# Turning the banded heads' probabilities by DMA transposes instead of TensorE, in a hybrid attention layer

## The chip, the cores and the metric

The kernel runs on one core of one Trainium2 chip. The metric is the device time of one execution in microseconds. The profile is of one such execution, taken by the hardware profiler; stated times are from runs of the kernel by itself.

## The reference

One decoder layer, 2048 positions of width 1024. The input is normalised, modulated and projected once; eight heads do attention over all earlier positions with a forget gate ("forgetting heads", mixer A), eight heads do attention within a band of 128 positions with a learned sink ("banded heads", mixer B, two key/value heads). Both are gated, concatenated, projected, normalised and added to the input. The change touches mixer B:

```python
def sliding_window_sink_attention(q, k, v, sinks):
    qb = q.reshape(B, nb, Q_BLOCK, SWA_KV_HEADS, SWA_GROUP, d)
    kk, vv = with_prev(k), with_prev(v)          # this block of 128 and the one before
    s = jnp.einsum('bnqhgd,bnshd->bnhgqs', qb, kk) * (d ** -0.5)
    s = jnp.where(mask, s, -jnp.inf)             # band of 128
    p = jax.nn.softmax(jnp.concatenate([s, sink], axis=-1), axis=-1)[..., :-1]
    return jnp.einsum('bnhgqs,bnshd->bnqhgd', p, vv)
```

## The kernel before, in words

Numbers are kept as pairs of float16 parts, high and low; a product of two such numbers is three matmuls (high by high, high by low, low by high), summed in PSUM.

The program has four stages one after the other: a prologue (normalising, keys and values of the banded heads), the banded heads, the forgetting heads, and the output projection. In the banded stage TensorE makes the remaining projections (`punits`, called by `fill`: each unit is three matmuls of 512 columns at L314, or twelve of 128 at L332) between the steps of 32 *pairs*. A pair (class `Pair`) is two neighbouring blocks of 128 queries of two heads, so eight 128×128 blocks of probabilities, or six where it holds the sequence's first block. For pair n:

- `scores` (L852): 12 matmuls into `pss`, a PSUM tile of two banks with one buffer (pool `ps_s`).
- `maxima` (L863, L865, L869): VectorE scales, masks and takes the row maxima into `sm_`; GpSimd (POOL) copies the sinks beside them; VectorE makes the four negative maxima `b_nb`.
- `exps` (L876): four exponentials on ScalarE in place, with sums.
- `turn` (L885): TensorE turns the eight float32 blocks into the PSUM tile `pxb` (two banks); ScalarE copies it, rounded, to the high half of `ptb` (L894), VectorE writes the low half (L890) and the reciprocals of the sums (L892). The two run one and two ticks later.
- `pv` (L904): 24 matmuls of turned probabilities with values into `pob`; VectorE scales them (`on`, L910), POOL's queue stores them to memory (`o_d`, L912).

The order of the instructions is written by hand (`manual_schedule`). Each engine runs its own in that order and waits only by semaphores. `tick()` runs what was put off with `after(n, ...)`, n ticks earlier. The loop over pairs, with three more ticks and the units of the projections dealt over four parts:

```python
            if n:
                windows[n - 1].pv()
            wd.turn()
            if n + 1 < NW:
                windows[n + 1].scores()
```

So the values of pair n-1 come one pair after its exponentials, and the scores of pair n+1 are the last thing that TensorE does in pair n. The projections share three PSUM banks `bk`; a bank goes back when ScalarE and VectorE have read it.

Query projections are rotated (`evac_rope`): ScalarE copies the bank to `qf`, four DMAs on SP's queue exchange its halves into `qs` (L712), VectorE reads that six ticks later (L725), and the rotated parts `stb` (pool `abp`, L719) are what `scores` reads. SP's queue also loads a piece of the output weights a pair (`wsq`, L1127), of which ScalarE takes a sum of squares (L1123). Between the banded and the forgetting heads, `key_limbs` (L1216 to L1222) on VectorE writes a small tile `lk`, which `key_rows` has TensorE turn (L1199).

Line numbers in the prediction are those of the kernel before.

Of the kernel before, what the change touches and what calls it, by code (L numbers as in the profile page):

```python
# [41 lines left out]
def hybrid_layer(  # L42
# [612 lines left out]
    def open_fox():  # L655
        nonlocal abp
        xlx.close()
        abp = swa_pool("abp", 4)
# [175 lines left out]
    class Pair:  # L834
# [20 lines left out]
        def maxima(self):  # L855
# [4 lines left out]
            m = sm(4, "b_m")  # L860
            for e, (i, k0, nk) in enumerate(self.blocks):
# [6 lines left out]
            self.nb = sm(4, "b_nb")  # L868
            V.tensor_scalar(self.nb[:], m[:], -1.0, LIFT, op0=ALU.mult, op1=ALU.add)  # L869

        def exps(self):
            self.rs = sm(4, "b_rs")
            for e, (i, k0, nk) in enumerate(self.blocks):
                for h in range(2):
                    p, c = self.sm_[:, e, h, :nk * P + 1], slice(2 * e + h, 2 * e + h + 1)
                    A.activation(p, p, AF.Exp, bias=self.nb[:, c], accum_out=self.rs[:, c])  # L876

        def turn(self):

            nt = self.nt  # L880
            px = ps_t.tile([P, 8, P], F32, tag="t", name="pxb")
            for e, (i, k0, nk) in enumerate(self.blocks):
                for h in range(2):
                    for b in range(nk):
                        PE.transpose(px[:, self.at[e] + h * nk + b, :], self.sm_[:, e, h, b * P:(b + 1) * P], ident[:])  # L885
# [3 lines left out]
            def low():  # L889
                V.tensor_tensor(lo, px[:, 0:nt, :], hi, op=ALU.subtract)  # L890
                self.rinv = sm(4, "b_ri")
                V.reciprocal(self.rinv[:], self.rs[:])  # L892

            after(1, lambda: A.activation(hi, px[:, 0:nt, :], AF.Copy))  # L894
            after(2, low)

        def pv(self):
            j, i = self.j, self.i
            po = ps_pv.tile([P, 4, 64], F32, tag="pv", name="pob")
            for e, (i_, k0, nk) in enumerate(self.blocks):  # L900
                for h in range(2):
                    for b in range(nk):
                        for n, (pp_, vv) in enumerate(((0, 0), (0, 1), (1, 0))):
                            PE.matmul(po[:, 2 * e + h, :], self.ptt[:, pp_, self.at[e] + h * nk + b, :],  # L904
# [177 lines left out]
    with swa_order:  # L1082
# [7 lines left out]
        wsp = swa_pool("wsp", 2)  # L1090
# [9 lines left out]
        for n, wd in enumerate(windows):  # L1100
# [8 lines left out]
            if n:  # L1109
                wd.exps()  # L1110
            fill(part[1])
# [20 lines left out]
        tick()  # L1132
# [506 lines left out]
```

## Time and profile before

| | us |
|---|---|
| median of 3 runs (1190.57 to 1196.38) | 1191.41 |
| the profiled execution | 1192.12 |
| its span in the profile | 1190.1 |
| mean granted clock of TensorE | 0.994 |
| banded stage, from 163 to 429 us | 266 |

The span is what the profiler saw of the execution, from its first to its last event; 2.0 us lie around it. Busy time of an engine is the union of its instructions. The chain is followed back from the last instruction, at each step to what released it. In lists of groups a row reads: line, engine, operation, out<-in, shapes, count | busy us, mean ns of one | idle time of the engine before them, and what ended it. A wait for several semaphores is put down to the one that came last by the profile.

### The profile page before, as it was taken

The page shows a single profiled execution, that of the slowest core. Times are in us where ns is not written, and L with a number is a line of the kernel's source. Part 1 is how long each engine was busy: PE and PEld are TensorE (multiplying, and loading weights), DVE is VectorE, ACT ScalarE, POOL GpSimd, SP SyncE. Part 2 cuts the span into 40 slices and gives each one's busy share as a digit, 9 for nine tenths or more (in the row PEclk, how much of TensorE's full clock was granted, in tenths as well). Part 3 has the DMA queues.
Part 4 walks back from the last instruction along what each step waited for, and adds up shares of the span by engine and source line. Part 5 has one row for each costly group of instructions (what it writes and reads, how often), then busy time and mean ns, then how long its engine had stood idle before and what let it go on. Part 6 is the DMA issues. An engine that isn't in the chain of part 4 may idle for free.

```text
span 1190.1 us, 27190 instructions
## 1 busy us (share of the span) xinstructions
PE 1146.8 (96%) x10829; PEld 690.1 (58%) x10829; DVE 912.6 (77%) x2261; ACT 665.0 (56%) x1100; POOL 115.2 (10%) x231
## 2 busy tenths in 40 slices
PE   5899999999999998999999999999999999999997
PEld 2465556765568976455555555555555555555553
DVE  7877677777777749588888899887888887766665
ACT  2784346465555511476666666666666778433332
POOL 2000122112222211011000101001000000000000
PEclk9899999999999999999999999999999999999999
DMA  9745443223233332423425332223311345455652
GB/s 331 265 133 90 98 85 89 59 80 90 85 86 72 53 74 53 60 63 87 68 70 81 94 60 63 47 48 77 41 42 41 90 129 174 147 174 181 202 168 90
DMA packets 87579, 120.22 MB, mean 101 GB/s; under 512 B 27508, under 2 KB 63388, under 8 KB 87452
## 3 DMA queue, kind: packets, MB, share of 16 engines
q1 hardware_dynamic: 76184, 85.69, 24.8%
q0 software_dynamic: 10832, 32.50, 13.5%
q8 instruction: 85, 1.39, 0.7%
q14 instruction: 42, 0.34, 0.2%
q10 hardware_dynamic: 436, 0.28, 0.1%
HBM read 71.04 MB, written 25.18 MB: 81 GB/s over the span
## 4 chain that ended last, share of the span: by engine, by line
PE 80%; DVE 10%; DMA 5%; ACT 2%; issue 2%; SPq 1%; DVEq 0%; ACTq 0%
PE bk L314 30%; PE bk L1448 13%; PE bk L332 7%; PE sta L1292 4%; PE sta L1291 4%; PE bk L1242 4%; PE poa L1317 2%; PE poa L1318 2%; PE poa L1315 2%; PE pxb L885 2%; DMA wa<-in_w_ada_dram 2%; PE pss L852 2%; DVE a_m L1245 2%; PE pob L904 2%; DMA sinT<-sn__241 1%
## 5 line engine op out<-in xcount | busy, mean ns | idle before, releaser
L1298 ACT ACTIVATE p<-sta,lift,scl_qk 128x1024 f32<-128x1024 f32 (+2 forms) x160 | 171.9, 1074 | 143.8 <-PE sta L1292 88.0
L314 PE MATMUL bk<-hT,wh_qk 128*128 128x512 f16 x768 | 195.8, 381 | 0.0
L1245 DVE TENSOR_REDUCE a_m<-bk 128x1 f32<-128x512 f32 x192 | 130.3, 685 | 58.1 <-PE bk L1242 56.9
L1448 PE MATMUL bk<-wohl,oz 128*128 128x512 f16 x768 | 172.2, 379 | 0.7 <-DVE oz L1435 0.7
L1305 DVE TENSOR_TENSOR pha<-p,pha 128x1024 f16<-128x1024 f32 (+2 forms) x160 | 169.0, 1057 | 0.2 <-ACT pha L1302 0.2
L1302 ACT ACTIVATE pha<-p 128x1024 f16<-128x1024 f32 (+2 forms) x160 | 148.1, 925 | 8.5 <-PE bk L1242 3.1
L1448 PEld LDWEIGHTS <-oz 128*128 128x128 f16 x768 | 74.2, 99 | 82.3 <-DVE oz L1435 2.8
L314 PEld LDWEIGHTS <-wh_qk 128*128 128x128 f16 x768 | 72.6, 98 | 78.2 <-issue 6.8
L1318 PE MATMUL poa<-vt,pha 128*128 128x65 f16 x1088 | 116.0, 192 | 1.4 <-DVE pha L1305 1.2
L1315 PE MATMUL poa<-vt,pha 128*128 128x65 f16 x1088 | 116.5, 193 | 0.5 <-DVE ona L1324 0.4
L1317 PE MATMUL poa<-vt,pha 128*128 128x64 f16 x1088 | 116.5, 194 | 0.0
L1291 PE MATMUL sta<-T 128*128 128x512 f16 (+1 forms) x320 | 110.9, 346 | 2.4 <-ACT p L1298 2.4
L1242 PE MATMUL bk<-T 66*128 66x512 f16 (+2 forms) x320 | 109.9, 349 | 3.4 <-DVE a_m L1245 3.2
L1315 PEld LDWEIGHTS <-pha 128*128 128x128 f16 x1088 | 101.5, 96 | 15.0 <-DVE ona L1324 1.5
L1292 PE MATMUL sta<-T 69*128 69x512 f16 (+1 forms) x320 | 109.8, 348 | 0.0
L1317 PEld LDWEIGHTS <-pha 128*128 128x128 f16 x1088 | 100.9, 97 | 11.4
L1318 PEld LDWEIGHTS <-pha 128*128 128x128 f16 x1088 | 100.8, 99 | 1.8 <-DVE pha L1305 1.7
L314 PE MATMUL bk<-hT,wh_za 128*128 128x512 f16 x384 | 99.7, 378 | 0.0
L332 PE MATMUL bk<-wh_va,hT 128*128 128x128 f16 x1536 | 90.7, 219 | 0.0
L332 PEld LDWEIGHTS <-hT 128*128 128x128 f16 x1536 | 87.5, 98 | 4.7 <-issue 2.1
L314 PE MATMUL bk<-hT,wh_zb 128*128 128x512 f16 x384 | 89.2, 379 | 0.0
L314 PE MATMUL bk<-hT,wh_qb 128*128 128x512 f16 x384 | 87.4, 379 | 0.0
(490 smaller groups left out, 1846.7 us busy)
## 6 DMA issues: line engine op xcount, KB each, us to landing
hT<-in_x_dram SPq DMA_DIRECT2D x20, 512.0 KB
wa<-in_w_ada_dram SPq DMA_DIRECT2D x16, 512.0 KB
z_d<-tz POOLq DMA_DIRECT2D x32, 256.0 KB, 3.0
T<-stq SPq DMA_DIRECT2D x64, 128.0 KB
T<-o_d SPq DMA_DIRECT2D x16, 512.0 KB
T<-z_d SPq DMA_DIRECT2D x16, 512.0 KB
out_dram<-hT SPq DMA_DIRECT2D x15, 512.0 KB
xt<-in_x_dram SPq DMA_DIRECT2D x12, 512.0 KB
```

The lines of the kernel that those rows point to most:

```text
L314: PE.matmul(ps, whl[:, a, k, :], hT[ci][:, b, k, :], start=(k == 0 and n == 0), stop=(k == KT - 1 and n == 2))
L332: PE.matmul(ps[:, u * P:(u + 1) * P], hT[ci][:, a, k, u * P:(u + 1) * P], whl[:, b, k, :], start=(k == 0 and n == 0), stop=(k == KT - 1 an ...
L1242: PE.matmul(mx[:, :w], T[0:XM, 0, i * P:(i + 1) * P], T[0:XM, 2, pc * CH:pc * CH + w], start=True, stop=True)
L1245: V.tensor_reduce(m3[:, u, pc:pc + 1], mx[:, :w], axis=AX.X, op=ALU.max)
L1291: PE.matmul(self.st[:, o:o + w], T[:, 3, kb_], T[:, 1, qc], start=True, stop=False)
L1292: PE.matmul(self.st[:, o:o + w], T[0:XR, 2, kb_], T[0:XR, 0, qc], start=False, stop=not diag)
L1298: A.activation(self.p32[:, :self.w], self.st[:, :self.w], AF.Exp, scale=scl[f"qk{self.hd}"][:], bias=lift[:])
L1305: V.tensor_tensor(self.ph[:, 1, :self.w], self.p32[:, :self.w], self.ph[:, 0, :self.w], op=ALU.subtract)
L1315: PE.matmul(po[:, u, :], ph[:, 0, pq], vt[:, b, hd, 0:65], start=(self.first and n == 0 and u == 0), stop=False)
L1317: PE.matmul(po[:, u, 0:64], ph[:, 0, pq], vt[:, b, hd, 65:VW], start=False, stop=False)
L1318: PE.matmul(po[:, u, :], ph[:, 1, pq], vt[:, b, hd, 0:65], start=False, stop=(self.last and n == len(self.blocks) - 1))
L1448: PE.matmul(py, self.hl[:, i, k, :], w_slot(8 * j + k)[:, cc], start=(k == 0 and m_ == 0), stop=(k == KT - 1 and m_ == 2))
```

## The change

1. `turn` on TensorE goes, and with it the PSUM tile `pxb`. ScalarE rounds the exponentials to float16 from SBUF (`high`), right after the exponentials; VectorE takes the rest (`low`), at the end of the pair. Each part has a tile `pr` of its own from the pool `stp`, which has two.
2. Each part is turned by one DMA transpose from SBUF to SBUF on SP's queue, `turn(0)` and `turn(1)`, into a tile `ptb` of its own. The pool `ptp` has five such tiles of half the size, where it had one of the whole size.
3. The values come two pairs later (`windows[n - 2].pv()`), where it was one.
4. `pss` has two buffers, and the scores of pair n+1 are made before the last quarter of pair n's projections and before the values.
5. `b_nb` is made in two halves, one after each block's maxima. The pool `abp` has three tiles for four, `wsp` one for two.
6. `key_limbs(1)` runs two units earlier, before the end of the projections between the stages.

```diff
+                nb = sm(2, "b_nb")
+                V.tensor_scalar(nb[:], m[:, 2 * e:2 * e + 2], -1.0, LIFT, op0=ALU.mult, op1=ALU.add)
+                self.nb.append(nb)
-            self.nb = sm(4, "b_nb")
-            V.tensor_scalar(self.nb[:], m[:], -1.0, LIFT, op0=ALU.mult, op1=ALU.add)
...
-        def turn(self):
-            nt = self.nt
-            px = ps_t.tile([P, 8, P], F32, tag="t", name="pxb")
-            for e, (i, k0, nk) in enumerate(self.blocks):
-                for h in range(2):
-                    for b in range(nk):
-                        PE.transpose(px[:, self.at[e] + h * nk + b, :], self.sm_[:, e, h, b * P:(b + 1) * P], ident[:])
-            self.ptt = ptp.tile([P, 2, 8, P], F16, tag="pt", name="ptb")
-            hi, lo = self.ptt[:, 0, 0:nt, :], self.ptt[:, 1, 0:nt, :]
...
-                V.tensor_tensor(lo, px[:, 0:nt, :], hi, op=ALU.subtract)
...
-            after(1, lambda: A.activation(hi, px[:, 0:nt, :], AF.Copy))
-            after(2, low)
+        def high(self):
+            self.pr = [stp.tile([P, 8, P], F16, tag="st", name="pr") for _ in range(2)]
+            self.ptt = []
+            for p32, hi in self.parts(0):
+                A.activation(hi, p32, AF.Copy)
+
+        def low(self):
+            for p32, hi, lo in self.parts(1):
+                V.tensor_tensor(lo, p32, hi, op=ALU.subtract)
+            self.rinv = sm(4, "b_ri")
+            V.reciprocal(self.rinv[:], self.rs[:])
+
+        def turn(self, n):
+            self.ptt.append(ptp.tile([P, 8, P], F16, tag="pt", name="ptb"))
+            SP.dma_start_transpose(self.ptt[n][:, 0:self.nt, :], self.pr[n][:, 0:self.nt, :].rearrange("p t c -> p (t c)"))
...
-        ptp = swa_pool("ptp", 1)
-        ps_s = swa_pool("ps_s", 1, space=PSUM)
-        ps_t = swa_pool("ps_t", 1, space=PSUM)
+        ptp = swa_pool("ptp", 5)
+        ps_s = swa_pool("ps_s", 2, space=PSUM)
...
             if n:
                 wd.exps()
+            wd.high()
             fill(part[1])
             tick()
             fill(part[2])
             tick()
-            fill(part[3])
-            if n:
-                windows[n - 1].pv()
-            wd.turn()
+            wd.turn(0)
             if n + 1 < NW:
                 windows[n + 1].scores()
+            fill(part[3])
+            if n > 1:
+                windows[n - 2].pv()
+            wd.low()
+            wd.turn(1)
...
+            if pos[0] >= N_V3 - 2 and not limbs1:
+                key_limbs(1)
+                limbs1 = True
             tick()
-        key_limbs(1)
```

TensorE's instructions at the end of one pair, before the change (`pob` is the values' result, `pxb` the turned blocks, `pss` the next pair's scores, `bk` a bank of the projections; rows that repeat are left out):

```order
L314 MATMUL bk0_137<-hT0_107,wh_zb2_3392 128x512
L904 LDWEIGHTS ptb_3469
L904 MATMUL pob_3550<-vb_565,ptb_3469 128x64
...
L885 MATMUL pxb_3575<-ident_116,sm__3492 128x128 x8
L852 LDWEIGHTS stb_2920
L852 MATMUL pss_3585<-kst0_563,stb_2920 128x256
...
L314 LDWEIGHTS wh_qb2_3203
L314 MATMUL bk2_139<-hT1_108,wh_qb2_3203 128x512
```

The same place after it, where `ptb_3383` and `ptb_3438` are the two turned parts of a pair two back:

```order
L314 MATMUL bk2_139<-hT1_108,wh_qb2_3171 128x512
L852 LDWEIGHTS stb_3179 [waits Activation_49]
L852 MATMUL pss_3604<-kst0_563,stb_3179 128x256 [waits DVE_49]
...
L314 MATMUL bk1_138<-hT1_108,wh_zb2_3352 128x512
L915 LDWEIGHTS ptb_3383 [waits DMAHW2_49]
L915 MATMUL pob_3632<-vb_565,ptb_3383 128x64 [waits DVE_49]
...
L915 LDWEIGHTS ptb_3438 [waits DMAHW3_49]
L915 MATMUL pob_3632<-vb_565,ptb_3438 128x64
```

The turns are gone, the scores stand before the last projections, and the values' weights now wait for DMAs.

SP's queue before, over some four pairs of the same stage:

```order
L1127 DMA wsq_2264<-in_w_out_dram 128x256 [waits Activation_49]
L712 DMA qs_2300<-qf_2299 32x512 [waits DMAHW1_49,DMAHW2_49,DMAHW0_49,DMAHW7_49,DVE_49,Activation_49]
L712 DMA qs_2300<-qf_2299 32x512 [waits DMAHW6_49]
L712 DMA qs_2300<-qf_2299 32x512 x2
L1127 DMA wsq_2387<-in_w_out_dram 128x256
L1127 DMA wsq_2497<-in_w_out_dram 128x256 [waits Activation_49]
L712 DMA qs_2519<-qf_2518 32x512 [waits DMAHW5_49,DMAHW3_49,DMAHW6_49,DMAHW0_49,DMAHW7_49,DVE_49,Activation_49]
```

And after, over two pairs:

```order
L906 DMA_TRANSPOSE ptb_3383<-pr_3349 128x8x128 [waits DMAHW2_49,PE_49,Activation_49]
L906 DMA_TRANSPOSE ptb_3438<-pr_3350 128x8x128 [waits DMAHW3_49,DVE_49,PE_49]
L1140 DMA wsq_3441<-in_w_out_dram 128x256 [waits DMAHW4_49,Activation_49]
L712 DMA qs_3464<-qf_3463 32x512 [waits DMAHW5_49,DMAHW6_49,DVE_49,Activation_49]
L712 DMA qs_3464<-qf_3463 32x512
L712 DMA qs_3464<-qf_3463 32x512 [waits DMAHW7_49]
L712 DMA qs_3464<-qf_3463 32x512 [waits DMAHW0_49]
L906 DMA_TRANSPOSE ptb_3498<-pr_3481 128x8x128 [waits DMAHW1_49,PE_49,Activation_49]
L906 DMA_TRANSPOSE ptb_3551<-pr_3482 128x8x128 [waits DMAHW2_49,DVE_49,PE_49]
```

Two transposes a pair stand on the queue; the first waits for ScalarE's rounding, the second for VectorE's and for TensorE's values, which free its tile. The exchange `qs` and the load `wsq` stand behind them.

More of the change, by code (lines that the diff above doesn't have):

```diff
@@ L657, in open_fox @@
         xlx.close()
[L658 removed]
+        abp = swa_pool("abp", 3)
         early.close()
@@ L875, in exps, with parts @@
                     p, c = self.sm_[:, e, h, :nk * P + 1], slice(2 * e + h, 2 * e + h + 1)
[L876 to L895 removed]
+                    A.activation(p, p, AF.Exp, bias=self.nb[e][:, h:h + 1], accum_out=self.rs[:, c])
+        def parts(self, n):
+            same = self.blocks[0][2] == self.blocks[1][2]
+            for es in ([slice(0, 2)] if same else [slice(0, 1), slice(1, 2)]):
+                e, ne = es.start, es.stop - es.start
+                nk = self.blocks[e][2]
+                yield (self.sm_[:, es, :, 0:nk * P], *[
+                    pr[:, self.at[e]:self.at[e] + 2 * ne * nk, :].rearrange("p (e h b) c -> p e h (b c)", e=ne, h=2)
+                    for pr in self.pr[:n + 1]])
+        def high(self):
[11 more added lines that the diff above has]
+            SP.dma_start_transpose(self.ptt[n][:, 0:self.nt, :], self.pr[n][:, 0:self.nt, :].rearrange("p t c -> p (t c)"))
         def pv(self):
@@ L1132, in hybrid_layer @@
         tick()
+        windows[NW - 2].pv()
         fill(6)
```

6 lines of the change are left out of this document (4 added, 2 removed).

## The prediction

> **What bounds the kernel now.** I read the page first: its head, the shares of the engines and the chain that ended last, which say whether one engine sets the time.
>
> ```profile
> span 1190.1 us, 27190 instructions
> PE 1146.8 (96%) x10829; PEld 690.1 (58%) x10829; DVE 912.6 (77%) x2261; ACT 665.0 (56%) x1100; POOL 115.2 (10%) x231
> PE 80%; DVE 10%; DMA 5%; ACT 2%; issue 2%; SPq 1%; DVEq 0%; ACTq 0%
> ```
>
> TensorE (PE) is busy 96% of the span and holds 80% of the chain. That is a mean, and the change is in one stage, the 32 pairs of the banded heads. So the windows come next, over the stretch from the second pair's values (163 us) to the last but a few of its projections (429 us), and over three shorter stretches in it. Columns: PE, PEld, DVE, ACT, POOL busy, TensorE's clock, DMA share, GB/s.
>
> ```profile
> 163.00:429.00 266.00, 265.71 (x3175) 188.35 (x3174) 198.09 (x564) 143.77 (x392) 59.37 (x134) 1.00 0.34 79
> 172.00:181.00 9.00, 8.74 (x73) 4.66 (x72) 8.83 (x27) 4.39 (x13) 1.57 (x4) 1.00 0.38 74
> 189.00:198.00 9.00, 9.00 (x89) 5.39 (x86) 8.54 (x26) 5.45 (x15) 1.59 (x4) 1.00 0.33 103
> 198.00:206.00 8.00, 8.00 (x141) 7.22 (x139) 4.78 (x14) 5.06 (x14) 1.86 (x4) 1.00 0.55 148
> ```
>
> In this stage PE leaves 0.3 us of 266 idle, at full clock. VectorE (DVE) is busy 198.1 us, 74%, but nearly all of the time in the second and third rows. A pair takes 266/32 = 8.3 us. What is taken off PE here shortens the kernel until something else is late. The timeline of PE over one pair's end shows what can be taken off:
>
> ```profile
> 256.45 0.86 PE L904 MATMUL pob<-vb,ptb 128*128 128x64 f16 x24
> 257.15 1.07 PE L885 MATMUL pxb<-ident,sm__3492 128*128 128x128 f32 x8
> 258.15 0.83 PE L852 MATMUL pss<-kst,stb 64*128 64x256 f16 x12
> 258.91 5.35 PE L314 MATMUL bk<-hT,wh_qb 128*128 128x512 f16 x24
> ```
>
> The first column is the start, and matmuls overlap at their ends, so costs are taken from start to start: values 0.70 us, the eight turns 1.00 us, scores 0.76 us, then projections.
>
> **Part 1, PE's turns go.** How many there are is seen from the copies of their result:
>
> ```profile
> L894 ACT ACTIVATE ptb<-pxb x32: 810/1023/1023, 155.8 to 419.8; 128x1024 f16<-128x1024 f32 x28, 128x768 f16<-128x768 f32 x4
> ```
>
> 28 pairs turn eight blocks and four turn six: 28 x 1.00 + 4 x 0.77 (estimate: 1.00 x 6/8 and a little) = 31.1 us off PE. Nothing replaces them on PE: matmuls for scores and values stay. The new pair length is (266 - 31)/32 = 7.35 us.
>
> **Part 2, rounding to two halves.** It was read from PSUM (L894 on ACT, L890 on DVE); now both operands lie in SBUF. The nearest rows are the same operations of the other heads, L1302 and L1305.
>
> ```profile
> L1305 DVE TENSOR_TENSOR pha<-p,pha 128x1024 f16<-128x1024 f32 (+2 forms) x160 | 169.0, 1057 | 0.2 <-ACT pha L1302 0.2
> L1302 ACT ACTIVATE pha<-p 128x1024 f16<-128x1024 f32 (+2 forms) x160 | 148.1, 925 | 8.5 <-PE bk L1242 3.1
> L890 DVE TENSOR_TENSOR ptb<-pxb,ptb 128x1024 f16<-128x1024 f32 x28 | 34.1, 1216 | 0.0
> L869 DVE TENSOR_SCALAR b_nb<-b_m 128x4 f32<-128x4 f32 x30 | 5.3, 177 | 1.0
> ```
>
> DVE saves 32 x (1.22 - 1.06) = 5.1 us and pays for the second small b_nb of each pair 32 x 0.18 = 5.7 us: no change, 198 us in a stage of 235, 84%. ACT's copy takes about 0.93 for 1.02 us; ACT has 122 us to spare. Both at nothing, while DVE keeps up.
>
> **Part 3, the second score buffer.** DVE waits in this stage for two things, the values (L910) and after them the scores (L865). The second is put down to a copy on POOL:
>
> ```profile
> DVE on L910 <- PE pob L904: 21.8, 15, 3.0
> DVE sm__4426 L865 <- POOL sm__4426 L863: 1.4, 1, 1.4
> 316.21 0.42 DVE L910 TENSOR_TENSOR on<-pob,b_ri 128x256 f32<-128x256 f32 x1 [1.48 <-PE pob L904]
> 318.02 0.54 DVE L865 CUSTOM_DVE_ANT_0 sm__4426<-pss,bmask,snk 128x256 f32<-128x256 f32 x1 [1.39 <-POOL sm__4426 L863]
> 317.01 0.83 PE L852 MATMUL pss<-kst,stb 64*128 64x256 f16 x12
> 303.00 0.54 DVE L865 CUSTOM_DVE_ANT_0 sm__4185<-pss,bmask,snk 128x256 f32<-128x256 f32 x1
> 304.09 0.31 POOL L863 COPY sm__4185<-snk 128x2 f32<-128x2 f32 x2
> ```
>
> At 303.00 the maxima began before that tile's copy on POOL (304.09). So the copy is not what they wait for: at 318.02 it is the scores, which end at 317.84 because PE makes them last, after values and turns. With two buffers they are made a quarter of a pair's projections earlier, and this wait of up to 1.4 us a pair goes. The next thing late for DVE is the values alone, and to wait for those is to be ahead of PE. This is why I let DVE follow PE at 7.35 us. The price that stays: over the two dense windows DVE needs 8.83 and 8.54 us in stretches that shrink by 12% to 7.9, 1.6 us over in all, before a light one (4.78 of 8) lets it catch up. Three projection banks lie between. I take 2 us for such stalls, from 0 to 9 (the DVE rival).
>
> The scores need their turned queries earlier. The tightest pair had them 6.9 us ahead (end of the stb row to the pss row), and loses some 2 us of that.
>
> ```profile
> 174.39 0.69 DVE L719 TENSOR_TENSOR stb<-qc,stb 128x512 f16<-128x512 f32 x1
> 181.94 0.83 PE L852 MATMUL pss<-kst,stb 64*128 64x256 f16 x12
> ```
>
> **Part 4, the transposes on SP's queue.** 64 DMA transposes of 256 KB are new, two a pair, and no trace here has one. SP's queue holds in this stage the four qs exchanges of a query slice (14 slices) and one wsq load a pair. Rows: issues on SP, the z_d store of the same 256 KB (POOL, issue 0.56 us; 3.0 us to landing), and the queue's totals.
>
> ```profile
> 253.66 2.42 SPq L712 DMA_DIRECT2D qs<-qf  x4
> 256.12 1.70 SPq L1127 DMA_DIRECT2D wsq<-in_w_out_dram  x2
> L356 POOL DMA_DIRECT2D z_d<-tz x11 | 6.2, 564 | 41.7 <-DVE tz L354 41.6
> z_d<-tz POOLq DMA_DIRECT2D x32, 256.0 KB, 3.0
> q1 hardware_dynamic: 76184, 85.69, 24.8%
> ```
>
> SP now issues 2.42 x 14/32 + 0.85 = 1.9 us a pair. A transpose's issue time T is bounded below by 0.56 us (a plain issue of its bytes) and above by 4.84 us (each of its eight blocks at the price of a qs issue, 2.42/4 = 0.605). The queue keeps up while 2T + 1.9 is under 7.35 us, which is T under 2.7. I take 0.85, the wsq row, the one 128-partition issue on this queue; 0.85 and 2.7 give the same time. On the 16 DMA engines, q1's packets take 0.248 x 16 x 1190 = 4722 us: 62 ns a packet, or 55 us a MB. A transpose of 0.262 MB is then 0.90 us by bytes, and 4.0 us if it moves in 1024 pieces of 128 elements at a packet each. With the 0.34 x 8.3 = 2.8 us that the engines work now, a pair needs 4.6 to 10.8 us of 7.35. I take the low end, since its partition rows are 2 KB like z_d's.
>
> What waits for it: the values need both parts about two pairs (14.7 us) after the turn of the second; the rounding of the next pair needs its tile back in one (7.35 us). Landing as in z_d's row, 3.0 us, is hidden by PE's work of those pairs. SP itself now stops for ACT's rounding, DVE's rounding and PE's values; behind it stand the wsq load and the qs exchange, whose reader comes six ticks (two pairs) later: nothing.
>
> **A rule against the change.** The row above gives TensorE 1.00 us for eight f32 blocks, 0.125 us each in the stream. The Trainium skill (VectorE: DVE Perf Modes, "The three transpose paths") lists 390 ns for a 128×128 block on TensorE and 1309 ns by DMA; its first figure is not what this trace shows, and no run here shows the second. By it, blocks one after the other, the estimate is 16 x 1.309 = 20.9 us a pair and 1595 us in all. The skill (DMA: Bandwidth & Descriptors, "Latency and other measured facts") also has 261 GB/s for a transpose, by which 256 KB is an estimated 1.0 us and hidden.
>
> **Part 5, key_limbs.** PE stood 2.62 us for the key rows of the second forgetting head, whose six DVE instructions came behind three maxima:
>
> ```profile
> 474.49 1.88 DVE L1245 TENSOR_REDUCE a_m<-bk 128x1 f32<-128x512 f32 x3
> 476.29 0.23 DVE L1216 TENSOR_SCALAR a_cv<-csum,isc_qk 128x16 f32<-128x16 f32 x1
> 477.61 0.25 PE L1199 MATMUL bk<-identh,lk 128*72 128x128 f16 x1 [2.62 <-DVE lk L1219]
> ```
>
> They now run earlier. But DVE is the late one here, and the 1.3 us that they take delay the maxima and the banks that PE wants instead: 0 to -2.6, I take -1.
>
> **The sum.** -31.1 + 2 - 1 = -30.1 us, from the profiled execution's 1192.1: 1162.0 us. The median of the runs shown is 0.7 us below it. Its own range, with stalls from 0 to 9 us and limbs from -2.6 to 0: 1158 to 1170.
>
> **Rivals.**
> *DVE paces the stage.* If of DVE's 67.9 us idle only the 21.8 us for the values can go, the stage takes 198.1 + 46.1 = 244 us, a saving of 22: 1170, and up to 1180 if the dense windows stall too. For it: the two dense windows. Against: the waits for scores go as well.
> *The queue takes what PE gives.* If T is 3.2 us, a pair's queue is 2 x 3.2 + 1.9 = 8.3 us, its present length: within a few us of 1191. Decided by T between 3.0 and 3.4.
> *The queue is the bound, slower.* From T = 3.4 up, SP's issue sets the pair. At 4.84 us it is 11.6 us: 3.3 x 32 = 105 us more, 1297. By the DMA engines' pieces 10.8 us: 80 more, 1272. For it: pieces of 256 bytes, as a block's row is, are small beside the mean packet (85.69 MB/76184 = 1.1 KB). Against: one instruction a part, and 2 KB rows. The skill's rule of 1309 ns a block belongs here, as its far end.
>
> **How the numbers follow.** The forecast 0.50; DVE's pace 0.16; the queue takes it all 0.11; slower by the queue 0.23, of which 0.08 for blocks in series and 0.05 for T so near the point that it ends under 1215. A run of this kernel can be told from no change from about 0.5%, 6 us, on: faster is below 1185, slower above 1197. So faster 0.66, same 0.11, slower 0.23. The range 1156 to 1215 holds the first three cases and the mild part of the fourth, about 0.8; its middle is not the forecast.
>
> **What would show it.** Right: the stage shorter by 28 to 31 us with PE still busy all through, no L885, L865 without waits for scores, SP busy under 7 us a pair, values waiting for no transpose. Wrong: PE idle before the values (L915) for a DMA, a transpose issue over 2.7 us, or DVE busy without a gap while PE waits for banks. A gain without a shorter banded stage would refute all of it.

## The result, and the profile after

The changed kernel is slower by 1.1%. Its median is 1208.19 us (1205.36 to 1209.14, 4 runs); the kernel before, run beside it, took 1192.73 us (1190.57 to 1196.38, 4 runs). The ratio is 1.0113, with a 95% interval of 1.0096 to 1.0130. The forecast was 1162 us. Some executions run at a lower clock throughout and take longer: such runs (one of e13's four, one of e18's) are left out of the times and ratios here, and a ratio is taken from the other runs of both kernels, so it can differ by 0.2% from the quotient of the medians. The profiled execution took 1207.8 us, of which 1205.9 are its span. Below are the head of the page, its shares, the share of the 16 DMA engines in 40 slices of the span, the totals of SP's queue, and the chain.

```profile
span 1205.9 us, 26884 instructions
PE 1133.7 (94%) x10581; PEld 668.4 (55%) x10581; DVE 916.7 (76%) x2297; ACT 668.5 (55%) x1104; POOL 115.3 (10%) x231
...
DMA  9746477949597952333424421222311336445552
...
q1 hardware_dynamic: 141720, 101.95, 35.3%
...
PE 56%; issue 14%; DVE 13%; DMA 10%; ACT 3%; POOL 2%; SPq 1%; DVEq 0%; POOLq 0%; ACTq 0%
```

The 248 turns are off PE (10581 matmuls for 10829), and yet PE holds 56% of the chain where it held 80%; DMA and "issue" took its place. The DMA engines' digits are 4 to 9 from the sixth slice to the fifteenth, which is the stage of the banded heads. SP's queue moved 65,536 packets more than before: 1024 on the mean for each of the 64 transposes.

The windows over the stage, first of the kernel before and then of the changed one, have the same columns as in the prediction (PE, PEld, DVE, ACT, POOL busy, TensorE's clock, DMA share, GB/s):

```profile
140.00:430.00 290.00, 289.71 (x3335) 200.56 (x3334) 212.33 (x599) 153.97 (x419) 62.73 (x142) 1.00 0.34 81
```

```profile
140.00:430.00 290.00, 264.61 (x2860) 166.66 (x2859) 207.09 (x607) 153.70 (x412) 57.41 (x134) 0.96 0.77 129
```

PE now idles 25 us of 290 and its clock is 0.96 on the mean. The share of the DMA engines went from 0.34 to 0.77. The last values start at 430.4 us before and at 444.3 us after: the stage ends 14 us later where about 30 us less was forecast. What follows takes 761.6 us after and 759.7 before, so 14 of the 16 us of the span lie here. The waits between 140 and 450 us say who stands for what (total, times, longest, in us), and then those of PE.

```profile
...
ACT wsq L1136 <- DMA wsq<-in_w_out_dram: 29.8, 12, 7.3
ACT pr L895 <- DMA ptb<-pr: 27.1, 9, 6.1
...
DVE pr L899 <- DMA ptb<-pr: 24.7, 9, 7.4
POOL mxr L226 <- DMA mx_d<-w_mx: 19.4, 5, 7.3
...
DVE on L921 <- PE pob L915: 2.1, 2, 1.8
```

```profile
PE bk L332 <- issue: 7.0, 4, 3.4
PE pob L915 <- DVE on L921: 6.8, 2, 3.6
PE bk L314 <- ACT wh_zb L252: 4.1, 2, 2.1
```

ACT and DVE stand for rounded tiles that a transpose is still reading, and ACT stands for wsq, the load behind the transposes on SP's queue. PE waits for no transpose. Part of its idle time is for what ACT and DVE bring late: the projections' weights (`wh`, 12.4 us in all, of which the third row is the largest) and the values' PSUM tile, which DVE has not read yet. 7.0 us are put down to "issue", at the projections of 128 columns: there PE waited for nothing that the profile shows.

One pair end to end, from the timeline of ACT, DVE and SP's queue:

```profile
270.84 1.06 ACT L895 ACTIVATE pr<-sm__3560 128x1024 f16<-128x1024 f32 x1
271.92 2.97 SPq L906 DMA_TRANSPOSE ptb<-pr  x2
271.93 1.23 DVE L899 TENSOR_TENSOR pr<-sm__3560,pr 128x1024 f16<-128x1024 f32 x1 [0.40 <-ACT pr L895]
...
279.35 1.06 ACT L895 ACTIVATE pr<-sm__3674 128x1024 f16<-128x1024 f32 x1 [2.36 <-DMA ptb<-pr]
...
280.93 1.23 DVE L899 TENSOR_TENSOR pr<-sm__3674,pr 128x1024 f16<-128x1024 f32 x1 [0.45 <-DMA ptb<-pr]
283.11 0.42 ACT L1136 ACTIVATE wsq<-wsq 128x256 f32<-128x256 f32 x1 [2.69 <-DMA wsq<-in_w_out_dram]
```

The first transpose is issued at 271.92 and the second right behind it, for DVE rounds the second part as soon as ACT has rounded the first. The first tile comes back at 279.3, 7.4 us later, and the second at 280.9, for which the chain has 7.58 us from 273.26 on:

```profile
273.26 7.58 DMA ptb<-pr
```

Only then do ACT and DVE round the next pair, and after that ACT stands again, for wsq.

### The profile page after: what moved, and what is told of

Read it like the earlier page. It is cut to its first block, busy times and chain, and to the rows that moved or that the text cites. A ratio compares the mean times of both kernels' runs of the same rounds, so it can differ in the third digit from the quotient of the medians.

```text
span 1205.9 us, 26884 instructions
## 1 busy us (share of the span) xinstructions
PE 1133.7 (94%) x10581; PEld 668.4 (55%) x10581; DVE 916.7 (76%) x2297; ACT 668.5 (55%) x1104; POOL 115.3 (10%) x231
## 4 chain that ended last, share of the span: by engine, by line
PE 56%; issue 14%; DVE 13%; DMA 10%; ACT 3%; POOL 2%; SPq 1%; DVEq 0%; POOLq 0%; ACTq 0%
PE bk L314 19%; PE bk L1462 13%; PE sta L1306 4%; PE sta L1305 4%; PE bk L1256 4%; PE poa L1331 2%; PE poa L1332 2%; PE poa L1329 2%; DMA wa<-in_w_ada_dram 2%; DVE a_m L1259 2%; DMA ptb<-pr 2%; DMA mx_d<-w_mx 2%; PE bk L332 1%; DVE pha L1319 1%; PE bk L1421 1%
## 5 line engine op out<-in xcount | busy, mean ns | idle before, releaser
L332 PE MATMUL bk<-wh_va,hT 128*128 128x128 f16 x1536 | 97.5, 223 | 13.5 <-issue 7.0
L332 PEld LDWEIGHTS <-hT 128*128 128x128 f16 x1536 | 91.2, 100 | 19.3 <-issue 17.1
L314 PE MATMUL bk<-hT,wh_zb 128*128 128x512 f16 x384 | 95.3, 394 | 5.1 <-ACT wh_zb L252 4.1
L314 PE MATMUL bk<-hT,wh_qb 128*128 128x512 f16 x384 | 89.9, 381 | 1.4 <-DVE wh_qb L258 1.4
```

The costliest lines, as they stand in the source:

```text
L314: PE.matmul(ps, whl[:, a, k, :], hT[ci][:, b, k, :], start=(k == 0 and n == 0), stop=(k == KT - 1 and n == 2))
L332: PE.matmul(ps[:, u * P:(u + 1) * P], hT[ci][:, a, k, u * P:(u + 1) * P], whl[:, b, k, :], start=(k == 0 and n == 0), stop=(k == KT - 1 an ...
```

## Experiments

Five theories were on the table. A: with two tiles for rounded parts, ACT and DVE stand until the transposes have read them. B (later G): the transposes load the 16 DMA engines, and every transfer lands later. C: their issue is slow on SP. D: the new order itself makes ACT or DVE late. E (later F): wsq has a single buffer, or stands behind the transposes on SP's queue.

### The price of one transpose (e1)

The program leaves the whole computation out. It times transposes and plain copies of 256 KB by a DVE read of the result, alone, and transposes also beside a load of 512 KB. Shortened:

```
for n in range(4):
    SP.dma_start_transpose(dst[0], src[0]); look(dst[0])    # alone
    ...
    G.dma_start(big[n], w_in0[...])                         # 512 KB
    SP.dma_start_transpose(dst[8], src[0]); SP.dma_start_transpose(dst[9], src[0])
```

> Computes nothing of the layer: it writes zeros, then times DMA transposes of 128x1024 float16 (256 KB) from SBUF to SBUF alone, in twos, eight in a row and beside a 512 KB load, and plain copies of the same bytes. Theory A (the tiles: what costs is that ScalarE and VectorE stop until a rounded tile's transpose has landed, while the transfer itself is ordinary): one transpose alone lands about 3 us after its issue, like the 256 KB stores of the layer, and eight in a row come at under 2 us each. Theory B (the transfer is slow: 256-byte pieces): one alone takes 4 us or more, two together 7 us or more, and eight in a row 4 us each; the plain copy is under half of that. Theory C (the issue is slow on SP): SP's issue of one takes over 2.7 us.

In these rows of DVE's timeline the bracket is the wait from the issue to the landing: of a transpose alone, a plain copy alone, a transpose of one 128x128 block, and a transpose beside the load.

```profile
34.06 0.16 DVE L68 COPY see<-dst 128x1 f16<-128x1 f16 x1 [3.14 <-DMA dst<-src]
...
44.60 0.16 DVE L68 COPY see<-dst 128x1 f16<-128x1 f16 x1 [2.40 <-DMA dst<-src]
...
55.96 0.16 DVE L68 COPY see<-dst 128x1 f16<-128x1 f16 x1 [2.31 <-DMA dst<-src]
...
101.43 0.16 DVE L68 COPY see<-dst 128x1 f16<-128x1 f16 x1 [6.63 <-DMA dst<-src]
```

Alone, a transpose lands in 3.14 us, near the 3.0 us that the prediction took, and eight in a row landed between 77.78 and 87.21 us, one each 1.35 us. Beside one load of weights it lands in 6.6 us. C is not it: in the changed kernel an issue takes 1.25 us (the middle one of least, median and most, in ns), far from the 3.0 to 3.4 from which it would decide.

```profile
L906 SPq DMA_TRANSPOSE ptb<-pr x64: 3/1248/3272, 154.1 to 437.8; - x64
```

B is not it either while nothing else moves; it can be when something else does. The kernel has such loads all through the stage.

### Copies in place of transposes (e2)

```
-            SP.dma_start_transpose(self.ptt[n][:, 0:self.nt, :], self.pr[n]...)
+            SP.dma_start(self.ptt[n][:, 0:self.nt, :], self.pr[n][:, 0:self.nt, :])
```

> The changed kernel with each DMA transpose replaced by a plain DMA copy of the same tile to the same tile, so the probabilities are not turned; all waits, queues and tiles stay. Theory A: a plain copy lands sooner, the waits for rounded tiles shrink, and the time falls well below the changed kernel's 1208, to 1165-1185 us. Theory B: the same fall, since the pieces are 2 KB. Theory D (no matter how fast the transfer is: the hand-over through SP's queue, one wsq buffer and the new order of the instructions make ScalarE and VectorE late): 1200-1210, unchanged.

1181.95 us, ratio 0.9946 (0.9928 to 0.9964). The order, the buffers and the places on SP's queue are those of the changed kernel, and the bytes are the same. The probabilities are not turned. That its ratio is 1.7% below the changed kernel's puts some 20 us on what a transpose has over a copy, its longer landing and its smaller pieces included. The waits for rounded tiles shrink from 51.8 us to 18.6:

```profile
ACT pr L895 <- DMA ptb<-pr: 11.0, 8, 2.7
ACT wsq L1136 <- DMA wsq<-in_w_out_dram: 9.1, 6, 2.5
DVE pr L899 <- DMA ptb<-pr: 7.6, 3, 3.6
```

### Four rounded tiles, then two buffers for wsq (e3, e4)

```
-    stp = swa_pool("stp", 2)
+    stp = swa_pool("stp", 4)       # room: the cosine table cut to 512 columns, 12 small loads of the prologue go
-        wsp = swa_pool("wsp", 1)
+        wsp = swa_pool("wsp", 2)   # e4 alone
```

> The changed kernel with four tiles for rounded parts (pool stp) instead of two. To find the 4 KB a partition, the table of cosines is cut to its first 512 columns, which every slice then uses, so the rotation is wrong, and 12 small table DMAs of the prologue are left out. Theory A: ScalarE's and VectorE's waits for landed transposes (51.8 us together in the changed kernel) go almost entirely, and the time falls to 1165-1185 us. Theory B: the transfers are as slow as before; the waits move to the values or to SP's issue, and the time stays at 1200-1210.

> As the kernel with four tiles for rounded parts, and with two buffers for the pieces of output weights (pool wsp) as the kernel before had. Theory A: a few us at most beyond the kernel with four tiles. Theory E (ScalarE stops 29.8 us for the single wsq buffer, and that is what makes the banks and weights late): the four tiles alone change little, this one falls to 1165-1185.

With four tiles 1189.61 us, ratio 0.9999 (0.9985 to 1.0014); with the second wsq buffer as well 1188.88 us, ratio 1.0002 (0.9981 to 1.0024). The stands for rounded tiles are gone, so A is true for a part: against the changed kernel's 1.0113 it is 1.1%, some 13 us. The time lies between what A (1165 to 1185) and B (1200 to 1210) had it at. Another stand has taken their place, and the second buffer does not take it away (e3, then e4):

```profile
ACT wsq L1137 <- DMA wsq<-in_w_out_dram: 58.6, 18, 6.2
```

```profile
ACT wsq L1137 <- DMA wsq<-in_w_out_dram: 59.0, 17, 6.8
```

E in its form "one buffer" falls.

### Without wsq, and without transposes (e5, e6)

e5 is e3 without the loads and squares of wsq. e6 is the changed kernel without transposes:

```
-            self.ptt.append(ptp.tile([P, 8, P], F16, tag="pt", name="ptb"))
-            SP.dma_start_transpose(self.ptt[n][:, 0:self.nt, :], self.pr[n]...)
+            self.ptt.append(ptc)        # one tile, filled once
```

> As the run with four rounded tiles, and the loads of wsq and ACT's squares of them are left out (the sum of squares is a constant, so the later scale of the output rows is not the reference's). If the stand of ACT for wsq (58.6 us there) is what still holds the banks back (F), that stand goes and nothing takes its place: the windows 140 to 430 hold 285 us of PE or more and the time is 1165 to 1172. If the engines are simply too loaded by the transposes' pieces (G), another load is late instead, the weights or the exchanges: PE stays near 275 of 290 and the time is 1182 to 1190.

> The changed kernel with no transposes at all: the turned tile is filled once with a constant and all values read it, so the banded heads' output is not the reference's. The rest of the order, the two rounded halves, the second score buffer and wsq stay. If the order and the hand-over are sound (all the loss is the transposes'), this is the forecast's own time, 1158 to 1170, with PE 286 us or more busy in the windows 140 to 430. If the new order itself makes ACT or DVE late (D), it stays at 1180 or above, and PE shows waits for banks and weights although nothing waits for a transpose.

e5 took 1187.05 us, ratio 0.9977 (0.9959 to 0.9995). The largest stand of all goes, and with it only 0.2% of the time: 59 us of ACT's idle time held up little. F falls. e6 took 1168.15 us, ratio 0.9821 (0.9798 to 0.9844). D falls too: without transposes the new order gives 1.8%, some 21 of the 30 us that were forecast. Its window, and the idle stretches of PE in it that are over 1.1 us:

```profile
140.00:430.00 290.00, 281.19 (x3199) 180.97 (x3198) 224.46 (x663) 160.00 (x430) 65.47 (x146) 1.00 0.33 84
```

```profile
220.43 2.28 PE L332 MATMUL bk<-wh_va,hT 128*128 128x128 f16 x38 [2.70 <-issue]
244.71 0.61 PE L314 MATMUL bk<-hT,wh_zb 128*128 128x512 f16 x2 [1.75 <-ACT wh_zb L252]
299.50 3.63 PE L314 MATMUL bk<-hT,wh_qb 128*128 128x512 f16 x16 [1.15 <-DVE wh_qb L258]
386.76 2.46 PE L332 MATMUL bk<-wh_va,hT 128*128 128x128 f16 x41 [1.14 <-issue]
```

PE is idle 8.8 us of 290. Of the 6.7 us in these four stretches, 2.9 are for projection weights that ACT and DVE round, and 3.8 are "issue". The 8.8 us are the upper end (9 us) of the stalls that the prediction allowed.

### Another queue for wsq, and tiles shared out otherwise (e7, e8)

```
-            SP.dma_start(wsq[n][:], w_out0[...])
+            G.dma_start(wsq[n][:], w_out0[...])               # e7 and e8
-        ptp = swa_pool("ptp", 5)
+        ptp = swa_pool("ptp", 3)                              # e8
+        prp = swa_pool("prp", 2)                              # rounded tiles of odd pairs
-            if n > 1:
-                windows[n - 2].pv()
+            if n:
+                windows[n - 1].pv()
```

> The changed kernel with the wsq loads issued by POOL on its own queue; all else as it was. If wsq lands late because it stands behind the transposes on SP's queue (F), ACT's 29.8 us for wsq fall to under 8, and the time falls by 5 to 15 us, to 1193 to 1203; the waits for rounded tiles stay. If it lands late because the 16 engines are full (G), the waits for wsq stay near 25 us and the time stays at 1206 to 1210.

> Nothing left out: values one pair behind, three tiles for turned parts, the room of the other two given to two more rounded tiles (even pairs use one pool, odd pairs the other), wsq loads on POOL's queue. If the waits for rounded tiles and for wsq are what made the change slow, 1168 to 1182. If the transposes land too late for values one pair behind (4.8 to 7.6 us against a pair of 7.4 us), PE stands before its values (L915) for ptb, some 1 to 3 us a pair, and it is 1190 to 1230. If the engines are the bound (G): 1185 to 1195, with the waits spread over weights and exchanges.

e7: 1202.61 us, ratio 1.0100 (1.0072 to 1.0128); ACT's stand for wsq fell from 29.8 to 8.1 us. So wsq did land late because of its place behind the transposes, but that is worth little (the interval touches that of the changed kernel). e8: 1205.74 us, ratio 1.0128 (1.0088 to 1.0167). Here PE does wait for the transposes, in 15 places, since the values come one pair behind:

```profile
PE pob L915 <- DMA ptb<-pr: 23.2, 15, 5.2
```

### Transposes that nobody reads (e9), one part (e10), every other pair (e11)

e9 is e6 with the 64 transposes back in their places, from the constant tile into four tiles that no instruction reads. e10 is the changed kernel with the first part transposed and the second part's turned tile a constant. e11 turns odd pairs on PE, as the kernel before did, with nothing left out.

```
             self.ptt.append(ptc)
+            junk = ptj.tile([P, 8, P], F16, tag="pj", name="ptj")           # e9
+            SP.dma_start_transpose(junk[:, 0:self.nt, :], ptc[:, 0:self.nt, :]...)
...
+            if n % 2 == 0:                                                  # e11
                 wd.low()
                 wd.turn(1)
+            else:
+                wd.on_pe()
```

> The kernel whose turned tile is filled once (1168 us, no transposes), with the 64 transposes put back at their places, from that constant tile into four tiles that nobody reads; no engine waits for any of them, and SP stands for none of ACT's or DVE's roundings. If the load of the DMA engines is what costs (G), the time goes up to 1180 to 1190, ACT stands for wsq again by 40 us or more, and weights' maxima (mxr) and exchanges land late. If the cost lay in standing for the transposes' landing (A), it stays at 1166 to 1172.

> The changed kernel with only the first part transposed, 32 transposes for 64; the second part's turned tile is a constant (the banded heads' output is not the reference's), its rounding is still made. If the cost goes with the load in proportion, half way between none and all: (1168 + 1208)/2 = 1188. If there is a knee where the engines' work still fits into a pair (G with slack: 0.33 + 0.22 = 0.55 of their time), 1168 to 1176. If any transpose in the loop costs its landing in order (A), 1195 or more.

> Nothing left out: even pairs as in the changed kernel by DMA transposes, odd pairs turned by PE from float32 as in the kernel before, values two pairs behind for both, one score buffer (its banks go to the turned scores). PE pays 16 x 1.0 us of turns. If the load of the engines has a knee, 1168 + 16 = 1184 or a little under, 1178 to 1186, faster than both. If the cost is in proportion to the transposes, the two even out: 1186 to 1198.

e9: 1191.84 us, ratio 1.0007 (0.9986 to 1.0028), 1.9% above e6. Nobody waits for these transposes, and SP's waits have no row for their four target tiles, so this is what they cost by being issued and in flight. Its window, then SP's queue in 140 to 430 us (packets, MB, share of the 16 engines), for e9 and for e6:

```profile
140.00:430.00 290.00, 270.01 (x3056) 175.35 (x3055) 215.47 (x633) 158.64 (x424) 62.00 (x142) 0.97 0.85 135
```

```profile
q1 hardware_dynamic: 73392, 24.81, 62.6%
```

```profile
q1 hardware_dynamic: 8694, 9.15, 12.4%
```

By the time of its packets one transpose takes all 16 engines (62.6% - 12.4%) x 290 / 64 = 2.27 us, and two make 4.5 us of a pair of 7.4. This is not a price by itself: in e1, with nothing else moving, one landed each 1.35 us, so packets take longer beside others. Other transfers land later too, though not all: between 140 and 430 us the median landing of a weight load (wr_va, four of them) is 7.5 us for 5.0 in e6 and of an output store (o_d) 5.0 for 3.7, but that of z_d, a store of 256 KB, is 2.9 for 3.0. The longest delay is in a round trip of the weights' maxima: POOL stores 0.5 KB (L221) and waits for it before it loads it back (L226). These are the same two steps of the same weight, in e6 and in e9:

```profile
274.12 0.55 POOL L221 DMA_DIRECT2D mx_d<-w_mx  x1 [1.88 <-DVE w_mx L218]
...
282.15 0.57 POOL L226 DMA_DIRECT2D mxr<-mx_d  x1 [4.09 <-DMA mx_d<-w_mx]
```

```profile
277.57 0.55 POOL L221 DMA_DIRECT2D mx_d<-w_mx  x1 [1.88 <-DVE w_mx L218]
...
292.03 0.57 POOL L226 DMA_DIRECT2D mxr<-mx_d  x1 [8.30 <-DMA mx_d<-w_mx]
```

It is 7.5 us from the end of the store's issue to the load's in e6 and 13.9 us in e9, and the weights can be rounded only after it. e10: 1185.29 us, ratio 0.9945 (0.9926 to 0.9964); against the same 32 transposes unread (e17 below, 0.9850), reading them, and standing for them, costs 1.0%. Its time lies in none of the three forecasts, nearest to the one in proportion. e11: 1188.39 us, ratio 0.9987 (0.9967 to 1.0008), no difference from the kernel before that can be told; that is the case in proportion.

### The earlier key_limbs alone (e12)

```
+            if pos[0] >= N_V3 - 2 and not limbs1:
+                key_limbs(1)
+                limbs1 = True
             tick()
-        key_limbs(1)
```

> The kernel before with only the earlier key_limbs of the second forgetting head. By the 2.62 us that PE stands there, up to 2.6 us less; by my step, 1 us less: 1187 to 1190 against 1190. If DVE's maxima are pushed into the banks that PE needs, no change or up to 1 us more.

1188.69 us against 1190.52, ratio 0.9985 (0.9975 to 0.9995): 0.6 to 3.0 us less.

### Bytes, pieces or the turning itself (e13 to e18)

All six put transfers that nobody reads into e6, at the same places. Plain copies are of 256 KB; the pieces of 256 bytes come from a target whose blocks lie 260 bytes apart.

```
             self.ptt.append(ptc)
+            junk = ptj.tile([P, 8, P + 2], F16, tag="pj", name="ptj")
+            SP.dma_start(junk[:, 0:self.nt, 0:P], ptc[:, 0:self.nt, :])     # e15: two a pair; e18: three
```

> As the run with unread transposes, with plain copies of the same 256 KB in their places, two a pair. They move the same bytes; by the run with plain copies (q1 at 29.3% for 24.8%) one takes the 16 engines about 0.8 us where a transpose takes 2.0. If the time of the engines that the pieces take is what costs, 1168 to 1176. If the bytes, or SP's queue with two more entries before wsq, are what costs, 1184 to 1192 as with the unread transposes.

> The same with five plain copies a pair, 160 in all, whose estimated time on the engines, 5 x 0.8 = 4.0 us a pair, is about that of two transposes (4.1). If it is the engines' time whatever fills it, 1184 to 1196 and a DMA share of 0.75 or more in the windows 140 to 430. If it is something of the transposition itself (its small pieces between the others' packets), under 1178 at the same share.

> Two unread plain copies a pair of the same bytes, into tiles whose blocks lie 260 bytes apart, so that they move in pieces of 256 bytes without being turned. If the small pieces are what costs, q1 has some 65,000 packets more, as with the transposes, the share of the engines in the windows 140 to 430 is 0.8 and the time 1186 to 1194. If it is the transposition itself, the packets are as many and the time is that of plain copies, 1172 to 1179.

> Eight unread plain copies a pair, 256 in all, so that the engines are as full as the transposes make them at their worst (share about 0.95). If the fullness of the engines decides, 1186 or more. If whole rows of 2 KB let others' transfers pass however many they are, 1174 to 1182.

> One unread transpose a pair, 32 in all (the first part's). In proportion, half of the 24 us that 64 cost: 1178 to 1182. With a knee, since the engines are then at about 0.58: 1168 to 1174.

> Three unread copies a pair in 256-byte pieces that are not turned, 96 in all. At 1.56 us of all 16 engines each (from the run with two), q1 would be at 12.4% + 96 x 1.56 / 290 = 64% in the windows 140 to 430, the place of two transposes (62.6%). If the engines' time is what costs, whatever fills it, the time is 1186 to 1200. If transposition does something more to other transfers, it is 1174 to 1181.

SP's queue in the same window, for e14, e15, e16, e17 and e18 (of e13 no row is used):

```profile
q1 hardware_dynamic: 30834, 49.00, 53.6%
```

```profile
q1 hardware_dynamic: 73177, 25.35, 46.8%
```

```profile
q1 hardware_dynamic: 38769, 63.43, 67.6%
```

```profile
q1 hardware_dynamic: 41358, 17.21, 34.6%
```

```profile
q1 hardware_dynamic: 105214, 33.35, 61.8%
```

| in flight beside e6's transfers, a pair | q1's share | time, us | ratio to before (95%) |
|---|---|---|---|
| none (e6) | 12.4% | 1168.2 | 0.9821 (0.9798 to 0.9844) |
| one transpose (e17) | 34.6% | 1171.8 | 0.9850 (0.9834 to 0.9867) |
| two copies, whole rows (e13) | - | 1174.9 | 0.9879 (0.9859 to 0.9899) |
| two copies, 256-byte pieces (e15) | 46.8% | 1173.5 | 0.9857 (0.9834 to 0.9880) |
| five copies, whole rows (e14) | 53.6% | 1176.8 | 0.9882 (0.9862 to 0.9902) |
| three copies, 256-byte pieces (e18) | 61.8% | 1176.6 | 0.9883 (0.9858 to 0.9909) |
| two transposes (e9) | 62.6% | 1191.8 | 1.0007 (0.9986 to 1.0028) |
| eight copies, whole rows (e16) | 67.6% | 1243.0 | 1.0457 (1.0422 to 1.0493) |

Copies of either kind cost 0.4% to 0.6% up to a share of 62%. Two transposes, at the same share as e18 and with fewer packets, cost 1.9%. So theory G in its plain form, that the engines' time is what counts whatever fills it, does not hold; neither bytes nor small pieces explain it. e16 is slowest of all at a like load (0.84 of the engines over all queues, 0.85 in e9, 0.83 in e18). There SP stands for its four target tiles before further copies, and ACT stands 119.5 us for wsq behind them. That this makes it slow, and not the load, is argued and not tested: SP also stands 59.9 us in e14, which costs 0.6%, and no run gives the copies of e16 more targets.

```profile
SPq L908 <- DMA ptj<-ptb: 78.9, 75, 5.4
```

So two transposes a pair cost three times what copies of equal engine time cost (e9 for e18). Late landings alone do not tell the two apart. The round trip shown above takes 8.0 us in e18, but 11.1 in e14, and e14's median landings of wr_va and o_d (6.8 and 4.7 us) are nearly those of e9, at a third of its cost.

What PE loses in e9 can be counted. It idles 20.0 us of 290 for 8.8 in e6, and its clock of 0.97 for 1.00 is worth some 9 us more (estimate: 0.03 x 290). Together that is 20 us, and its last values start 20.8 us later than e6's (432.3 for 411.5). These are PE's largest waits between 140 and 450 us in e9, in e6 and in e18:

```profile
PE bk L332 <- issue: 10.9, 6, 3.3
PE pob L916 <- DVE on L922: 3.6, 1, 3.6
PE bk L314 <- ACT wh_zb L252: 3.4, 2, 2.1
```

```profile
PE bk L332 <- issue: 4.2, 3, 2.7
PE bk L314 <- ACT wh_zb L252: 1.8, 1, 1.8
```

```profile
PE bk L332 <- issue: 4.6, 3, 2.2
PE bk L314 <- ACT wh_zb L252: 3.5, 2, 3.1
```

The weights are no later in e9 than in e18. What grew is the value tile that DVE had not read (once) and, most of all, "issue", which is 4.0 us in e17, 1.4 in e15 and 1.9 in e14. What PE stands for there the profile does not name, and it stays open; so does why the second transpose costs so much more than the first (1171.8, then 1191.8). One candidate that no run tested is PE's own instructions. The page counts a queue "instruction" (q8) on the same 16 engines, with 83 packets here and 85 in the kernel before, one for some 255 of PE's matmuls and weight loads in both. In e9 two of the six stretches (2.0 and 2.4 us) begin exactly 256 such instructions apart, and in both PE goes on 1.4 to 1.5 us after a packet of that queue has been moved. This would cover 4.4 of the 10.9 us.

## Why the prediction was wrong

**The account.** In ratios to the kernel before, the forecast stood at 1162.0/1191.41 = 0.9753. Without transposes it is 0.9821 (e6), with transposes that nobody reads 1.0007 (e9), and with those that are read, through two rounded tiles, 1.0113. The miss of 3.6% (43 us at 1191.41) is thus 0.7% (8 us) from stalls of the new order, 1.9% (22 us) from the transposes being in flight, and 1.1% (13 us) from their being read, with ACT and DVE standing for them; e3 gives the same last step from the other side (1.0113 to 0.9999).

**Part 1 was right in its mechanism, 9% too large.** The 248 turns went off PE. Its busy time is 1118.4 us in e6 for 1146.8 before, 28.4 us less where 31.1 were taken, and e6's last values start 18.9 us earlier than those of before (411.5 for 430.4).

**Part 2 was half right.** The rounding did not get cheaper from SBUF: 1.23 us on DVE and 1.06 us on ACT in the rows above, for 1.06 and 0.93 taken from the other heads' lines, and 1.22 and 1.02 before. DVE thus pays for the second small b_nb and saves nothing. This may be part of the 8 us; no run has it alone.

**Part 3 was right in its sign and short in its size.** The maxima waited for scores in some twenty pairs before, mostly for 1.2 to 1.6 us, and wait for none after. DVE's wait for values shrank from 26.4 us to 2.1 in the changed kernel (140 to 450 us), but for another reason than the forecast: DVE is no longer ahead there. The stalls were 8.8 us in e6, not 2, and at weights and in "issue"; no row puts any to banks behind dense windows.

**Part 4 is the step that failed.** It put at nothing what the transposes' own landing makes ACT and DVE wait for, which cost 13 us, and what transposes in flight do to the rest, which cost 22 us. Three of its sentences hold this.

- "I take the low end, since its partition rows are 2 KB like z_d's." The packets answer it: 1024 pieces a transpose, the other end of the bound. At about 32 ns a packet, (0.353 x 1205.9 - 0.248 x 1190.1) x 16 / 65,536, and not 62, they take 2.0 us of all engines over the whole run and 2.27 by e9, between 0.90 and 4.0. With 2.8 us of other work a pair needs 6.9 to 7.3 of 7.35 us (5.5 us by e1's 1.35 a transpose). The case was named, at 1272 us, and passed over; the term was put at less than half its size. It is not by itself what cost the time: e18 fills the engines as much and costs 0.6%.
- "Landing as in z_d's row, 3.0 us, is hidden". Alone it is 3.14 us (e1). In the pair shown it is 7.4 and 7.6 us, a whole pair, and with two rounded tiles ACT and DVE stand for the rest of it, 51.8 us in the stage. A landing that was read from the kernel before, with the engines at 0.34 in this stage, was used for a stage that the change itself brings to 0.77.
- "behind it stand the wsq load and the qs exchange, whose reader comes six ticks (two pairs) later: nothing." ACT stood 29.8 us for wsq. Its waits were only a sign, though: without wsq at all the time hardly moves (e5). Loads on POOL's queue land later too (wr_va 7.5 us for 5.0), and the transposes that nobody reads cost 22 us. Their price is idle time of PE and the clock that goes with it; for most of that idle time, the "issue", the cause stays open.

The issue, T, was in its bounds and harmless as said: 1.25 us for 0.85 taken.

**The rule against the change.** The list of transposes of the Trainium skill (VectorE: DVE Perf Modes, "The three transpose paths") has 1309 ns for a block by DMA; with the blocks taken one after the other, the prediction's far end by it was an estimated 1595 us. One block lands in 2.31 us and eight in 3.14, so a further block costs (3.14 - 2.31)/7 = 0.12 us: the blocks of one instruction are not in series at that price. The Trainium skill's other figure (DMA: Bandwidth & Descriptors, "Latency and other measured facts"), 261 GB/s, which the page gives for a middle dimension that is not contiguous, stands beside 262,144 bytes/1.35 us = 194 GB/s in e1. Neither price decided here; what the transposes do to the rest of the stage did.

**Part 5 was right.** -1 us was forecast, with 0 to -2.6; alone it measures -0.6 to -3.0 us (e12). It is the one piece of the change that is faster than the kernel before with nothing else lost. No version with the transposes and with nothing left out was shown to beat the kernel before.

**The rivals and the signs.** Of the three rivals, the one of the slower side came nearest: its place, the DMA engines, was right, but there they were to set the pair as a bound, and they were at 0.77 to 0.85. The range 1156 to 1215 holds the 1208 us by luck: its upper part stood for an issue of about 3.4 us, and the issue took 1.25 us. Of the signs of being wrong, PE stood for no DMA before the values, the issue passed 2.7 us once in 64 (3.27), and DVE was not without a gap (207.1 us busy of 290). The road by which the forecast failed was none of those named.

## What to carry to other kernels

Work that is moved from a full engine to the DMA engines is to be priced twice: by its landing beside the traffic that is there, and by what it does to that traffic. Add its engine time to the share that the stage has already, and take a sum near the stage's length as a warning rather than as a fit; but do not take the share as the price, since three kinds of transfer at 0.83 to 0.85 cost 0.6%, 1.9% and 6.5% here. The cheapest test comes first: the new transfers put into the kernel with nobody reading them, beside the kernel without them; here these two runs alone give two thirds of the loss that the order does not explain.

## What the hardware showed that was not expected

- A transpose of 128x1024 two-byte elements within SBUF takes 1024 packets on the mean. Back to back with nothing else moving, one lands each 1.35 us (e1). In the stage its packets' times add up to 2.0 to 2.3 us of all 16 engines; the same bytes in 256-byte pieces that are not turned take (46.8% - 12.4%) x 290 / 64 = 1.56 us, and in whole rows (53.6% - 12.4%) x 290 / 160 = 0.75 us.
- Two transposes a pair that nobody reads make the kernel slower than copies of equal engine time do (1191.8 for 1176.6 us); one a pair costs 0.3%, 3.6 us.
- In the changed kernel and in e9 TensorE's granted clock was lower in the stretches with most idle time of PE, which adds to the loss. The first row is a stretch of the changed kernel with 4.5 us idle in 20, the second the 3.4 us of e9 that come after PE's idle 3.6 us ahead of 294.48. It is no plain rule: in e6 PE idled 2.7 us ahead of 220.43 and its clock stayed at 1.00 (140 to 430 us).

```profile
220.00:240.00 20.00, 15.50 (x186) 10.97 (x183) 10.23 (x30) 7.94 (x26) 3.11 (x7) 0.83 0.81 93
```

```profile
293.90:297.30 3.40, 2.82 (x28) 1.82 (x28) 2.71 (x14) 1.62 (x7) 1.02 (x3) 0.50 0.97 132
```
